# A two-layer decoder on one core: the index scores of all DSA blocks ahead, the three selections behind the rest of the first stage

## The chip, the core and the metric

The kernel runs on one core of one Trainium2 chip. The metric is the device time of one execution in microseconds (us). The engines are named as in the profile: PE is TensorE (PEld its weight loads), DVE is VectorE, ACT is ScalarE, POOL is GpSimd, and SP is SyncE, which here only issues DMAs. Each engine works through its own queue in order; semaphores make one engine wait for another.

## The reference, cut to what matters

The reference is a decoder of two layers over 512 positions of width 1024. Each layer projects its input with one wide matrix and gives the columns to four mixers (`hgrn2`, `dsa`, `nsa`, `mlstm`); their outputs are joined and projected back, and cross-attention and a gated feed-forward follow. The change touches the `dsa` mixer only. For each block of 128 queries that mixer scores all keys with a small index network, keeps the 128 best keys of each query, and attends over those alone:

```python
topk = min(DSA_TOPK_MAX, l_ // 4)          # 128
def block(bi):
    rel = jax.nn.relu(jnp.einsum('bthd,bsd->bhts', iqb, ik))     # 8 index heads of 32
    score = jnp.einsum('bhts,bth->bts', rel, iwb).astype(F32)
    score = jnp.where(causal[None], score, -jnp.inf)
    _, idx = lax.top_k(score, topk)
    ...
```

A query of block 0 has at most 128 causal keys, so block 0 needs no selection. Blocks 1, 2 and 3 have 256, 384 and 512 causal keys to choose from.

## The kernel before, in words

The matrices are multiplied in split form: an operand is a pair of tiles, a rounded part and the rest (`xh` and `xl`, `wh` and `wl`), and a product is three matmuls. Weights come by DMA (`raw_tile`, L277), ACT makes the rounded part (L292) and POOL the rest (L293). In the second layer the first stage's weights come already split (L303).

`run` takes each layer through stages. The first stage holds, side by side, `dsa` (index scores and selections), `nsa_in` and `nsa`, `ml_in` and `ml`, and the projections `ml_in2`, `dsa_in2` and `hg_in`. The second stage holds `dsa_attn`, `hg` and the output projections; it reads the selections' masks, and its pools `hg`, `dat` and `xT` take the place of the first stage's pools `ml` and `nsa`.

Two things set the order of the work. First, the work is written as generators that are woven by `mix`: each part has a total, each `yield` names a cost, and the part whose spent share of its total is smallest goes on. `dsa` followed by `hg_space` is one part with a total of 74; everything else of the first stage is the other, with a total of 225. Second, Tile's planner lays out the queues (`schedule_with_timeline_sim=True`): what was emitted earlier has priority, and an engine that is free in its plan takes the best instruction that is ready then. `first()` moves weight loads, splits and some evictions far ahead. The queues that result are fixed in the program; on the chip an instruction that isn't ready holds up all behind it on its engine.

Inside `dsa`, for each block in turn, `index(tb)` makes the split query tile `iqs` (two ACT copies, one POOL subtract, L668 to L670), transposes it on PE into PSUM `dt` and copies it out as `iqT` (L497), then for each of 8 heads does one matmul (L679), one ACT relu into `rel` (L681) and one DVE pass that adds the weighted head into the score tile `iacc` (L684, L685, L688). `select(tb)` then runs 16 rounds on that tile: `max` finds the 8 largest of a row (L696) and `match_replace` overwrites them (L697); one more instruction makes the mask `dmask` (L700). There is one `iacc` tile (bufs=1), one `iqs` and one `iqT`, so a block's scores can only be added up once the selection before is done. The matmuls of `index` and its transposes share one PSUM bank, `dt`, through an alias.

After the selections `hg_space` closes the pool `dsa` and opens `hgin`. Only then may `hg_in` write its last two projections, `hgi` and `hgg`, into `h_v` and `h_g` (L485); it loops in `while self.hin is None` until then.

The last piece of the first stage is the last head of `ml`: four products into the single PSUM bank `mb` (L1048), each read by a DVE pass into `m_p` (L1056), then 20 matmuls (L1065), a chain of small DVE instructions on `m_den` (L1069 to L1079) and the output `mo`.

Of the kernel before, what the change touches and what calls it, by code (L numbers as in the profile page):

```python
# [7 lines left out]
FT = mybir.dt.float32  # L8
FR = mybir.dt.float32r
BF = mybir.dt.bfloat16  # L10
U8 = mybir.dt.uint8
AF = mybir.ActivationFunctionType
OP = mybir.AluOpType
# [193 lines left out]
class Kernel:  # L207
# [434 lines left out]
    def dsa(self, pool, keep):  # L642
        nc = self.nc
        idx = self.d_idx
        st = self.t(pool, "d_st", [128, 64], bufs=1)

        ik = idx[:, :, 256:288]
        self.sumsq(st[:, 4:8], ik, pool)
        self.rsqrt(pool, st[:, 8:12], st[:, 4:8], 1.0 / 32, EPS)
        self.tt(ik, ik, st[:, 8:12, None].to_broadcast([128, TB, 32]), OP.mult)  # L650
        self.tt(ik, ik, self.row("idxk_gain")[:, None, :].to_broadcast([128, TB, 32]), OP.mult)
        self.rope(idx[:, :, 256:288].rearrange("p t (h d) -> p t h d", h=1), self.ic, self.isn, 4, pool)
        iq = idx[:, :, 0:256].rearrange("p t (h d) -> p t h d", h=8)
        self.rope(iq, self.ic, self.isn, 4, pool)
        iks = self.t2(pool, "iks", [128, TB, 96], FR)
        nc.vector.tensor_copy(iks[:, :, 0:32], ik)
        nc.vector.tensor_copy(iks[:, :, 32:64], ik)
        self.tt(iks[:, :, 64:96], ik, iks[:, :, 0:32].bitcast(FT), OP.subtract)
        ikT = self.t(pool, "ikT", [128, S], FR, bufs=1)
        self.transpose_blocks(ikT[0:96], lambda j: iks[:, j, :].bitcast(FT), TB, nc.vector.tensor_copy, rows=96,  # L660
                              pool=pool)

        yield 4.0

        def index(tb):
            n = (tb + 1) * 128
            iqs = self.t(pool, "iqs", [128, 8, 96], FR, bufs=1)
            nc.scalar.activation(iqs[:, :, 0:32], iq[:, tb], AF.Copy)  # L668
            nc.scalar.activation(iqs[:, :, 64:96], iq[:, tb], AF.Copy)
            self.tt(iqs[:, :, 32:64], iq[:, tb], iqs[:, :, 0:32].bitcast(FT), OP.subtract, nc.gpsimd)  # L670
            iqT = self.t(pool, "iqT", [128, 8, 128], FR, bufs=1)
            for g in range(2):
                self.transpose_blocks(iqT[0:96, 4 * g:4 * g + 4].rearrange("p a b -> p (a b)"),
                                      lambda j: iqs[:, 4 * g + j, :].bitcast(FT), 4, self.act_copy, rows=96,
                                      pool=pool)
            acc = self.t(pool, "iacc", [128, S], bufs=1)[:, :n]
            for h in range(8):
                sc = self.psum("sc", pool=pool)
                nc.tensor.matmul(sc[:, :n], iqT[0:96, h], ikT[0:96, :n], start=True, stop=True)  # L679
                rel = self.t2(pool, "rel", [128, S])  # L680
                nc.scalar.activation(rel[:, :n], sc[:, :n], AF.Relu, scale=1.0 / 16)  # L681
                w = idx[:, tb, 288 + h:289 + h]
                if h == 0:
                    nc.vector.tensor_scalar(acc[:, :n - 128], rel[:, :n - 128], w, None, op0=OP.mult)  # L684
                    nc.vector.scalar_tensor_tensor(acc[:, n - 128:n], rel[:, n - 128:n], w, self.k("neg"),  # L685
                                                   op0=OP.mult, op1=OP.add)
                else:
                    nc.vector.scalar_tensor_tensor(acc, rel[:, :n], w, acc, op0=OP.mult, op1=OP.add)  # L688
                yield 0.7
            return acc  # L690

        def select(tb, acc, masks):
            n = (tb + 1) * 128
            m8 = self.t(pool, "m8", [128, 8])
            for r in range(16):
                nc.vector.max(m8, acc)  # L696
                nc.vector.match_replace(acc, m8, acc, -3e38)  # L697
                yield 0.4 + 0.25 * tb
            masks[tb] = self.t(keep, f"dmask{tb}", [128, n], BF, bufs=1)
            nc.vector.tensor_scalar(masks[tb], acc, -2e38, NEG, op0=OP.is_gt, op1=OP.mult)  # L700

        masks = self.d_masks = {0: None}
        for tb in range(1, TB):
            acc = yield from index(tb)
            yield from select(tb, acc, masks)

    def dsa_attn(self, pool):
        nc, l = self.nc, self.l
# [828 lines left out]
    def run(self):  # L1537
        nc = self.nc
        late = ExitStack()
        for l in range(DEPTH):  # L1540
            self.l = l
            banks = ExitStack()
            self.banks(banks, "ba", tp=1, sc=2, o=1, dt=1, mb=1)
            if l == 0:
                self.load_x(self.i["xT"])
            self.layer_consts()
            if l == 0:
                self.open_sq()
            right, index = ExitStack(), ExitStack()
            self.hqf = self.pool(right, "hgqf", side="right")  # L1550
            self.mo = {2: self.t(self.mp, "mo2", [128, 2, S], bufs=1), 3: self.t(self.mp, "mo3", [128, TB, 256], bufs=1)}
            pd = self.pool(index, "dsa", n2=4, n4=0, side="right")
            self.alias[id(pd)] = {"tp": "dt", "sc": "dt"}
            acc = self.dsa_in(pd)
            if l == 0:
                self.setup()
            self.rstd(row=True)
            if l == 0:
                xd = self.i["xT"]
            else:  # L1560
                xd = self.tc.dram_tile([D, S], FT, name=f"xd{l}")
                for c in range(KC):
                    nc.sync.dma_start(xd[c * 128:c * 128 + 128, :], self.xT[c])
            self.xpool.close()
            late.close()
            late, left = ExitStack(), ExitStack()
            pk = self.pool(late, "keep")
            pm = self.pool(left, "ml", n2=3)
            pn = self.pool(left, "nsa", n2=3, n4=1)
            self.alias[id(pn)] = {}  # L1570
            self.hin = None
            for tb in range(TB):
                with self.first():
                    nc.scalar.activation(self.d_idx[:, tb], acc[tb], AF.Copy, scale=self.rcol[:, tb:tb + 1])
            self.weave((self.chain(self.dsa(pd, pk), self.hg_space(index, right)), COST["dsa"]),
                       (self.chain(self.nsa_in(pn),
                                   self.mix((self.nsa(pn), COST["nsa"]),
                                            (self.chain(self.ml_in(pm),
                                                        self.mix((self.ml(pm), COST["ml"]),
                                                                 (self.chain(self.ml_in2(pm), self.dsa_in2(pk), self.hg_in()), COST["in"]))),  # L1580
                                             COST["mlin"]))),
                        COST["two"]))
            left.close()
            banks.close()
            banks = ExitStack()
            self.banks(banks, "bb", tp=1, sc=1, o=1, dt=1, hb=2)
            self.load_x(xd)
            ph = self.pool(left, "hg", n2=2, n4=0)
            pa = self.pool(left, "dat", n2=3, n4=0)
            px = self.pool(right, "xk", n2=2, n4=1, side="right")  # L1590
            self.alias[id(pa)] = {"tp": "dt"}
            self.attn_done = False
            self.weave((self.dsa_attn(pa), COST["attn"]), (self.hg(ph), COST["hg"]),
                       (self.chain(self.out_stage(0), self.xa_kv(px), self.out_stage(1)), COST["out"]))
            left.close()
            banks.close()
            banks = ExitStack()
            self.banks(banks, "bc", tp=2, sc=2, o=2)
            self.open_sq()
            with ExitStack() as e:  # L1600
                p = self.pool(e, "xa")
                rest = self.xa_in(p)
                right.close()
                self.raws = (self.pool(right, "raw", side="right"), RAWS)
                self.all(self.xa(p, self.pool(e, "xo", side="right"), rest))
            with ExitStack() as e:
                self.ffn(self.pool(e, "ffn"))
            self.raws = (self.wp, 3)
            right.close()
            banks.close()  # L1610
        self.xpool.close()
        late.close()
# [18 lines left out]
```

## Time and profile before

| what | value |
|---|---|
| time, median of 3 runs (lowest to highest) | 1689.66 us (1684.8 to 1689.67) |
| profiled execution: its time | 1688.9 us |
| profiled execution: its span | 1687.1 us |
| outside the span in that execution | 1.8 us |
| PE busy, share of the span | 1607.5 us (95%) |
| DVE busy | 924.0 us (55%) |
| ACT busy | 712.5 us (42%) |
| POOL busy | 799.1 us (47%) |
| mean granted TensorE clock | 0.972 |

The profile is one execution. Its page gives busy times, the span in 40 slices, and the groups of instructions; the trace behind it answers for any stretch, line or tile. A busy PE is not PE at its peak, since matmuls are pipelined and their ends are modelled. Idle time of an engine that isn't the bottleneck costs nothing. The granted clock is a share of full speed: 1.0 is 2.4 GHz, and half of that is the other level, 1.2 GHz; a mean between the two is a stretch that had both. In the trace the first stage of the first layer runs from about 25 to 277 us, that of the second layer from about 877 to 1115 us.

### The profile page before, as it was taken

How to read it: one execution, taken by the hardware profiler on the slowest of the kernel's cores; microseconds unless marked ns; L12 is line 12 of the kernel's file. 1: busy time of each engine (PE TensorE's matmuls, PEld its weight loads, DVE VectorE, ACT ScalarE, POOL GpSimd, SP SyncE). 2: the span in 40 equal slices, each digit the busy share in tenths (PEclk: the TensorE clock that was granted, in tenths of full speed). 3: DMA queues.
4: the chain of work that ended last, by engine and by line, in shares of the span. 5: the costliest groups of instructions: out<-in, count | busy, mean ns of one | idle time of the engine just before them, and what ended most of it. 6: DMA issues, size and time to landing. Idle time of an engine off the chain costs nothing.

```text
span 1687.1 us, 25484 instructions
## 1 busy us (share of the span) xinstructions
PE 1607.5 (95%) x9256; PEld 1333.1 (79%) x9262; DVE 924.0 (55%) x1760; ACT 712.5 (42%) x1525; POOL 799.1 (47%) x698
## 2 busy tenths in 40 slices
PE   7899998998899989999999999989998999999999
PEld 7778877777788868888898887677877888888887
DVE  5697688876755330344225884879786644123420
ACT  5555453454654443443324433423665433223321
POOL 5664333456448888874412010144672344444442
PEclk9999997999999999999999999979999999999999
DMA  5342212212338999953355734122131233333331
GB/s 160 89 119 76 70 34 84 57 38 85 112 121 286 305 316 319 333 192 93 105 156 178 262 107 132 58 95 57 45 119 38 66 97 90 92 100 94 94 103 66
DMA packets 114365, 212.72 MB, mean 126 GB/s; under 512 B 12984, under 2 KB 30136, under 8 KB 114240
## 3 DMA queue, kind: packets, MB, share of 16 engines
q1 hardware_dynamic: 111888, 206.11, 38.7%
q10 hardware_dynamic: 2032, 3.94, 0.7%
q8 instruction: 73, 1.20, 0.3%
q0 software_dynamic: 320, 1.05, 0.2%
q14 instruction: 52, 0.43, 0.1%
HBM read 170.69 MB, written 40.35 MB: 125 GB/s over the span
## 4 chain that ended last, share of the span: by engine, by line
PE 84%; DVE 8%; issue 3%; DMA 2%; POOL 2%; ACT 2%; SPq 0%; POOLq 0%; ACTq 0%; DVEq 0%
PE acc L329 14%; PE acc L331 14%; PE acc L330 14%; PE sc L330 5%; PE sc L331 5%; PE sc L329 5%; PE acc L339 3%; PE acc L340 3%; PE acc L341 3%; PE hb L856 3%; PE o L574 2%; PE sc L552 2%; PE tp L493 2%; PE mb L1048 1%; PE dt L493 1%
## 5 line engine op out<-in xcount | busy, mean ns | idle before, releaser
L293 POOL TENSOR_TENSOR wl<-wr,wh 128x512 fp32r<-128x512 f32 (+5 forms) x432 | 551.7, 1285 | 459.3 <-ACT wh L292 447.8
L292 ACT ACTIVATE wh<-wr 128x512 fp32r<-128x512 f32 (+5 forms) x432 | 252.1, 592 | 336.2 <-PE acc L330 149.2
L329 PE MATMUL acc<-xh,wh 128*128 128x512 f32 (+1 forms) x704 | 276.9, 395 | 0.8 <-ACT xh L1283 0.5
L330 PE MATMUL acc<-xl,wh 128*128 128x512 f32 (+1 forms) x704 | 274.6, 390 | 2.9 <-DVE xl L1277 2.9
L331 PE MATMUL acc<-xh,wl 128*128 128x512 f32 (+1 forms) x704 | 275.4, 392 | 0.4 <-POOL wl L293 0.4
L466 DVE TENSOR_TENSOR xT<-acc,xT 128x512 f32<-128x512 f32 (+1 forms) x112 | 68.1, 611 | 214.4 <-PE acc L331 213.6
L329 PEld LDWEIGHTS acc<-xh,wh 128*128 128x128 f32 x704 | 133.9, 191 | 32.1 <-issue 1.7
L330 PEld LDWEIGHTS acc<-xl,wh 128*128 128x128 f32 x704 | 134.3, 191 | 30.8 <-DVE xl L1277 4.0
L331 PEld LDWEIGHTS acc<-xh,wl 128*128 128x128 f32 x704 | 134.1, 190 | 28.7 <-POOL wl L293 1.1
L329 PE MATMUL acc<-f_gh,wh 128*128 128x512 f32 x352 | 139.1, 397 | 6.8 <-ACT f_gh L1491 6.8
L339 PE MATMUL acc<-wh,xh 128*128 128x256 f32 (+2 forms) x480 | 140.6, 296 | 4.9 <-DMA wh<-whl 3.8
L331 PE MATMUL acc<-f_gh,wl 128*128 128x512 f32 x352 | 139.7, 398 | 0.7 <-POOL wl L293 0.7
L330 PE MATMUL sc<-xl,wh 128*128 128x512 f32 x352 | 139.7, 397 | 0.0
L330 PE MATMUL acc<-f_gl,wh 128*128 128x512 f32 x352 | 139.5, 398 | 0.0
L340 PE MATMUL acc<-wl,xh 128*128 128x256 f32 (+2 forms) x480 | 139.0, 291 | 0.0
L331 PE MATMUL sc<-xh,wl 128*128 128x512 f32 x352 | 139.0, 395 | 0.0
L329 PE MATMUL sc<-xh,wh 128*128 128x512 f32 x352 | 138.0, 393 | 0.0
L341 PE MATMUL acc<-wh,xl 128*128 128x256 f32 (+2 forms) x480 | 137.4, 288 | 0.0
L318 POOL TENSOR_TENSOR phl<-pr,phl 128x512 fp32r<-128x512 f32 (+3 forms) x72 | 95.1, 1321 | 35.0 <-ACT phl L317 31.8
L317 ACT ACTIVATE phl<-pr 128x512 fp32r<-128x512 f32 (+3 forms) x72 | 44.2, 613 | 133.9 <-DMA pr<-in_wst 117.2
L339 PEld LDWEIGHTS acc<-wh,xh 128*128 128x128 f32 x480 | 92.9, 194 | 8.8 <-DMA wh<-whl 4.3
L340 PEld LDWEIGHTS acc<-wl,xh 128*128 128x128 f32 x480 | 93.3, 195 | 1.4 <-issue 0.8
(407 smaller groups left out, 3159.8 us busy)
## 6 DMA issues: line engine op xcount, KB each, us to landing
wr<-in_wst SPq DMA_DIRECT2D x332, 256.0 KB, 2.7
whl<-phl SPq DMA_DIRECT2D x52, 512.0 KB, 3.9
pr<-in_wst SPq DMA_DIRECT2D x52, 256.0 KB, 4.1
wh<-whl SPq DMA_DIRECT2D x52, 256.0 KB, 4.1
wl<-whl SPq DMA_DIRECT2D x52, 256.0 KB, 4.4
wr<-in_wst SPq DMA_DIRECT2D x48, 128.0 KB, 2.2
wr<-in_wst SPq DMA_DIRECT2D x32, 192.0 KB, 2.4
whl<-phl SPq DMA_DIRECT2D x8, 524.0 KB, 3.7
```

Of the source, the lines that this page charges most:

```text
L292: nc.scalar.activation(hi, raw, AF.Copy)
L293: nc.gpsimd.tensor_tensor(lo, raw, hi.bitcast(FT), op=OP.subtract)
L318: nc.gpsimd.tensor_tensor(both[:, 1], raw, both[:, 0].bitcast(FT), op=OP.subtract)
L329: self.nc.tensor.matmul(acc, wh, xh, start=(j == 0), stop=False)
L330: self.nc.tensor.matmul(acc, wh, xl, start=False, stop=False)
L331: self.nc.tensor.matmul(acc, wl, xh, start=False, stop=(j == n - 1))
L339: self.nc.tensor.matmul(acc, xh[:, s], wh, start=(first and j == 0), stop=False)
L340: self.nc.tensor.matmul(acc, xh[:, s], wl, start=False, stop=False)
L341: self.nc.tensor.matmul(acc, xl[:, s], wh, start=False, stop=(last and j == n - 1))
L466: self.nc.vector.tensor_add(self.xT[c][:, cols], acc, self.xT[c][:, cols])
L493: self.nc.tensor.transpose(p[:rows, j * 128:j * 128 + 128], src(j), self.ident)
L856: nc.tensor.matmul(sc[s0:s1, b + t0:b + t1], kk[po:po + 64, b + s0:b + s1], qq[po:po + 64, b + t0:b + t1], start=True, stop=True)
```

## The change: what it does

- `index` is called for blocks 1, 2 and 3 before any selection. Each block has a score tile of its own (`iacc1` to `iacc3`).
- `index` works in two halves of four heads: `iqs` and `iqT` are half as large, and `iqT` has two buffers. A head's `yield` is 0.5 in place of 0.7.
- After the last index head there is a `yield 60.0`. At that point `dsa` has spent 4 + 24 x 0.5 + 60 = 76 of its total of 74, so `mix` goes on with the other part until that has spent 76/74 of 225, which is 231.
- The 16 rounds follow, in each round blocks 1, 2 and 3 one after the other, each with its own `m8` tile; then the three masks.
- `hg_space`, and with it `hgi` and `hgg`, still comes behind the selections.
- The pool `dsa` has three buffers of the tag `t2` (`rel` and others) in place of four.

```diff
+        accs = {tb: self.t(pool, f"iacc{tb}", [128, (tb + 1) * 128], bufs=1) for tb in range(1, TB)}
+
         def index(tb):
             n = (tb + 1) * 128
-            iqs = self.t(pool, "iqs", [128, 8, 96], FR, bufs=1)
-            nc.scalar.activation(iqs[:, :, 0:32], iq[:, tb], AF.Copy)
-            nc.scalar.activation(iqs[:, :, 64:96], iq[:, tb], AF.Copy)
-            self.tt(iqs[:, :, 32:64], iq[:, tb], iqs[:, :, 0:32].bitcast(FT), OP.subtract, nc.gpsimd)
-            iqT = self.t(pool, "iqT", [128, 8, 128], FR, bufs=1)
+            acc = accs[tb]
             for g in range(2):
-                self.transpose_blocks(iqT[0:96, 4 * g:4 * g + 4].rearrange("p a b -> p (a b)"),
-                                      lambda j: iqs[:, 4 * g + j, :].bitcast(FT), 4, self.act_copy, rows=96,
-                                      pool=pool)
-            acc = self.t(pool, "iacc", [128, S], bufs=1)[:, :n]
-            for h in range(8):
...
-                yield 0.7
-            return acc
-
-        def select(tb, acc, masks):
-            n = (tb + 1) * 128
-            m8 = self.t(pool, "m8", [128, 8])
-            for r in range(16):
-                nc.vector.max(m8, acc)
-                nc.vector.match_replace(acc, m8, acc, -3e38)
-                yield 0.4 + 0.25 * tb
-            masks[tb] = self.t(keep, f"dmask{tb}", [128, n], BF, bufs=1)
-            nc.vector.tensor_scalar(masks[tb], acc, -2e38, NEG, op0=OP.is_gt, op1=OP.mult)
-
+
+                four = iq[:, tb, 4 * g:4 * g + 4]
+                iqs = self.t(pool, "iqs", [128, 4, 96], FR, bufs=1)
+                nc.scalar.activation(iqs[:, :, 0:32], four, AF.Copy)
+                nc.scalar.activation(iqs[:, :, 64:96], four, AF.Copy)
+                self.tt(iqs[:, :, 32:64], four, iqs[:, :, 0:32].bitcast(FT), OP.subtract, nc.gpsimd)
+                iqT = self.t(pool, "iqT", [128, 4, 128], FR, bufs=2)
+                self.transpose_blocks(iqT[0:96].rearrange("p a b -> p (a b)"), lambda j: iqs[:, j, :].bitcast(FT), 4,
+                                      self.act_copy, rows=96, pool=pool)
+                for h in range(4 * g, 4 * g + 4):
+                    sc = self.psum("sc", pool=pool)
+                    nc.tensor.matmul(sc[:, :n], iqT[0:96, h % 4], ikT[0:96, :n], start=True, stop=True)
...
+                    yield 0.5
+
+        for tb in range(1, TB):
+            yield from index(tb)
+
+        yield 60.0
+        for r in range(16):
+            for tb in range(1, TB):
+                m8 = self.t(pool, f"m8{tb}", [128, 8])
+                nc.vector.max(m8, accs[tb])
+                nc.vector.match_replace(accs[tb], m8, accs[tb], -3e38)
+                yield 0.05
         masks = self.d_masks = {0: None}
         for tb in range(1, TB):
-            acc = yield from index(tb)
-            yield from select(tb, acc, masks)
+            masks[tb] = self.t(keep, f"dmask{tb}", [128, (tb + 1) * 128], BF, bufs=1)
+            nc.vector.tensor_scalar(masks[tb], accs[tb], -2e38, NEG, op0=OP.is_gt, op1=OP.mult)
...
-            pd = self.pool(index, "dsa", n2=4, n4=0, side="right")
+            pd = self.pool(index, "dsa", n2=3, n4=0, side="right")
```

## Rows read from the trace of the kernel before

**Rows 1.** Windows: stretch, length, busy of each engine (instructions), clock, DMA share.
```profile
42.00:126.00 84.00, 72.87 (x512) 64.31 (x511) 65.39 (x143) 47.60 (x113) 52.05 (x39) 0.95 0.36 102
126.00:252.00 126.00, 124.93 (x825) 100.41 (x824) 93.06 (x193) 65.93 (x149) 47.44 (x38) 0.99 0.21 61
252.00:277.00 25.00, 17.88 (x85) 13.87 (x84) 22.80 (x60) 5.84 (x15) 3.81 (x5) 0.60 0.00 1
...
984.00:1092.00 108.00, 106.99 (x706) 85.17 (x706) 71.32 (x174) 40.83 (x95) 9.75 (x8) 1.00 0.29 96
1092.00:1115.00 23.00, 16.63 (x86) 14.47 (x87) 20.96 (x53) 6.49 (x16) 3.88 (x9) 0.70 0.01 1
```

**Rows 2.** Timeline of DVE: start, length; the last mask of each layer.
```profile
274.08 0.43 DVE L700 TENSOR_SCALAR dmask<-iacc 128x512 bf16<-128x512 f32 x1
...
1109.92 0.43 DVE L700 TENSOR_SCALAR dmask<-iacc 128x512 bf16<-128x512 f32 x1
```

**Rows 3.** Waits of PE from 252 to 277 us: total us, times, longest.
```profile
PE tp L1281 <- DVE mo L351: 2.5, 1, 2.5
PE mb L1048 <- DVE m_p L1056: 2.1, 2, 1.3
PE dt L723 <- DVE rs_ms L347: 1.0, 1, 1.0
```

**Rows 4.** Waits of PE from 1092 to 1115 us, the second layer's end.
```profile
PE mb L1048 <- DVE m_p L1056: 3.4, 2, 2.7
PE dt L1161 <- DVE mo L351: 1.9, 1, 1.9
PE mb L1048 <- DVE mo L351: 1.0, 1, 1.0
```

**Rows 5.** Timeline of PE: one head's 20 matmuls of L1065, at three places.
```profile
263.90 4.53 PE L1065 MATMUL mb<-m_v,m_p 128*128 128x65 f32 x20 [0.38 <-DVE m_p L1056]
...
1086.32 2.34 PE L1065 MATMUL mb<-m_v,m_p 128*128 128x65 f32 x20
...
1103.20 4.53 PE L1065 MATMUL mb<-m_v,m_p 128*128 128x65 f32 x20 [0.68 <-DVE m_p L1056]
```

**Rows 6.** Windows of line L696 alone (max): DVE busy (instructions), clock; the sum.
```profile
126.00:252.00 126.00, 12.42 (x22) 0.99 0.21 61
252.00:277.00 25.00, 7.59 (x11) 0.60 0.00 1
...
984.00:1092.00 108.00, 12.65 (x21) 1.00 0.29 96
...
sum 450.00, DVE 53.52; mean DVE 8.92
```

**Rows 7.** The same windows of line L697 alone (match_replace).
```profile
126.00:252.00 126.00, 13.58 (x42) 0.99 0.21 61
252.00:277.00 25.00, 8.23 (x22) 0.60 0.00 1
...
984.00:1092.00 108.00, 13.95 (x43) 1.00 0.29 96
...
sum 450.00, DVE 59.11; mean DVE 9.85
```

**Rows 8.** Timeline of POOL near the start: an instruction emitted late that runs early.
```profile
3.63 0.17 POOL L1222 MEMSET n_kbd<- 128x64 f32 x1
```

**Rows 9.** Waits of PE over the whole span, those on the index chain.
```profile
PE dt L679 <- ACT iqT L497: 3.2, 2, 2.6
PE dt L493 <- ACT rel L681: 3.1, 1, 3.1
...
PE dt L493 <- ACT iqT L497: 2.5, 2, 1.8
```

**Rows 10.** Two lines of DVE, whole span: count, shortest, median, longest ns.
```profile
L696 DVE MAX8 m<-iacc x96: 397/561/696, 79.5 to 1108.4; 128x8 f32<-128x256 f32 x32, 128x8 f32<-128x384 f32 x32, 128x8 f32<-128x512 f32 x32
...
L1008 DVE SCALAR_TENSOR_TENSOR m_y<-m_x,cols,m_y x24: 731/752/1872, 122.2 to 1065.9; 128x512 f32<-128x512 f32 x24
```

More of the change, by code (lines that the diff above doesn't have):

```diff
@@ L672, in index @@
-            for g in range(2):
-                self.transpose_blocks(iqT[0:96, 4 * g:4 * g + 4].rearrange("p a b -> p (a b)"),
-                                      lambda j: iqs[:, 4 * g + j, :].bitcast(FT), 4, self.act_copy, rows=96,
-                                      pool=pool)
-            acc = self.t(pool, "iacc", [128, S], bufs=1)[:, :n]
-            for h in range(8):
[L678 to L688, printed above, removed]
-                yield 0.7
@@ new lines, in index @@
+            for g in range(2):
+                four = iq[:, tb, 4 * g:4 * g + 4]
[9 more added lines that the diff above has]
+                    nc.tensor.matmul(sc[:, :n], iqT[0:96, h % 4], ikT[0:96, :n], start=True, stop=True)
+                    rel = self.t2(pool, "rel", [128, S])
+                    nc.scalar.activation(rel[:, :n], sc[:, :n], AF.Relu, scale=1.0 / 16)
+                    w = idx[:, tb, 288 + h:289 + h]
+                    if h == 0:
+                        nc.vector.tensor_scalar(acc[:, :n - 128], rel[:, :n - 128], w, None, op0=OP.mult)
+                        nc.vector.scalar_tensor_tensor(acc[:, n - 128:n], rel[:, n - 128:n], w, self.k("neg"),
+                                                       op0=OP.mult, op1=OP.add)
+                    else:
+                        nc.vector.scalar_tensor_tensor(acc, rel[:, :n], w, acc, op0=OP.mult, op1=OP.add)
+                    yield 0.5
```

## The prediction, made before the changed kernel was run

> **What bounds the kernel now.** I read the page first: PE is busy for 95% of the span and DVE for 55%. On average the kernel is bound by PE, and an edit to DVE's work is worth nothing unless some stage differs from the average. So I asked for windows. In the middle of the first stage PE is busy all the time and DVE has room: from 126 to 252 us PE works 124.93 of 126 us and DVE 93.06, and in the second layer, from 984 to 1092, PE 106.99 of 108 and DVE 71.32 [rows 1]. At the end of the stage the two change places: from 252 to 277 us DVE works 22.80 of 25 us and PE 17.88, from 1092 to 1115 DVE 20.96 of 23 and PE 16.63, and there alone the granted clock falls, to means of 0.60 and 0.70, between its two levels of 2.4 and 1.2 GHz [rows 1]. PE had waited in those stretches before it fell.
>
> What fills DVE there is the third selection: the last masks are made at 274.08 and 1109.92 us, 2.5 and 4.7 us before the stretches end [rows 2]. In the first layer 7.59 us of `max` and 8.23 us of `match_replace` lie in the 25 us of the tail, together 15.8 us [rows 6, 7]. They sit in DVE's queue between the last head's instructions. So PE waits for `m_p`, for `mo` and for a small `rs_ms`, 5.6 us in the largest three [rows 3], and in the second layer 6.3 us for `m_p` and `mo` [rows 4]. After the waits it runs at the lower clock: the 20 matmuls of L1065 take 4.53 us at either end and 2.34 us for the head before [rows 5].
>
> Why is the third selection so late? Block 3 can't add up its scores before block 2's selection has freed the one score tile, and its index work was emitted behind that selection.
>
> **The change part by part.**
>
> *Rounds out of the tail.* Nothing of the rounds is removed: 53.52 us of `max` and 59.11 us of `match_replace` in the two layers, so 56.3 us in each [rows 6, 7]. They are emitted last, so in the planner's list they are the filling for whatever DVE leaves free. That the planner does fill with work emitted far behind is seen at 3.63 us, where POOL clears a tile of `nsa_cmp` that is used much later [rows 8]. What room is there? In the middle of the first layer DVE's work other than rounds is 93.06 - 12.42 - 13.58 = 67.1 us, which leaves 126 - 67.1 = 58.9 us; in the second layer 71.32 - 12.65 - 13.95 = 44.7 us and 63.3 us [rows 1, 6, 7]. Both are above the 56.3 us wanted, and both are low counts: the score passes of blocks 2 and 3, which leave these stretches, are still in them, and from 42 to 126 us DVE has another 84 - 65.39 = 18.6 us idle [rows 1], open to the first blocks' rounds. Rounds beside a busy PE cost it nothing so far: 22 `max` and their partners lie in a stretch in which PE idles for 1.1 of 126 us [rows 1, 6]. So I take the rounds to be done before 252 and 1092 us, and their price in the middle as nothing. If the cover fails, each of the 96 wide instructions of a layer can push back what is queued behind it on DVE (the `stat` reduction that the attention's exponentials wait for, `m_p`, the evictions of `proj_T`) by up to its length; that is the second rival.
>
> The gain: the waits, 5.6 + 6.3 = 11.9 us [rows 3, 4], and the slowed L1065, 2 x (4.53 - 2.34) = 4.4 us [rows 5], together 16.3 us. The least is 0, if the bare chain of products and `m_p` makes PE wait as long and the clock falls all the same; the most is all of PE's idle time in the two stretches, (25 - 17.88) + (23 - 16.63) = 13.5 us, and the clock's share of its busy time, 0.40 x 17.88 + 0.30 x 16.63 = 12.1 us, together 25.6 us [rows 1]. I take 16.3, the sum of waits with a name.
>
> What is late next? The last head's own chain, and with it the second stage, whose pools wait for the first stage's. `hgi` and `hgg`, eight projections, stay behind `hg_space`; once the rounds are planned early, that pool opens early and they become filling for PE's holes in the tail. That is the way to the upper end.
>
> *Index work ahead.* Sixteen heads and 16 transposes of a layer move from the middle, where PE has no idle time, towards the front, where it idles for 84 - 72.87 = 11.1 us [rows 1]. PE's sum is the same. Part of that idle time is the index chain itself: at the passage from one block to the next PE waits 3.2, 3.1 and 2.5 us for `iqT` and `rel`, 8.8 us in the two layers [rows 9]. Now a second such passage, from block 2 to block 3, comes into the front, where there is less other work; against it, the halves are shorter and `iqT` has two buffers, so the next transposes need not wait for the last head. Bounds: the 8.8 us go, or they come twice. I take 0, and keep +/-8.8.
>
> *Smaller instructions.* 24 ACT copies of half the size and 12 POOL subtracts in place of 12 and 6 in the two layers: no row prices the halves, so at the most they cost what 12 and 6 more would; ACT has 84 - 47.60 = 36.4 us idle in the front and POOL 32.0 [rows 1]. Nothing. The `rel` pool of three buffers lets ACT run three heads ahead of DVE in place of four; the front's DVE time covers it. The change adds no DMA. SP's queue keeps its order; the loads of the second stage, gated by the first stage's last tiles, start earlier by what the tail loses.
>
> *POOL beside DVE.* A selection that moves from the tail, where POOL works 3.81 of 25 us, to the middle, where it works 47.44 of 126 [rows 1], could be slowed by it. The rows say no for the rounds: `max` ran 96 times between 397 and 696 ns at three widths, while the two-tile pass of L1008 has a median of 752 ns and a longest of 1872 [rows 10]. The Trainium skill (SBUF — State Buffer, section "Who interferes with whom") states the same split: a DVE instruction with two SBUF inputs can be shut out for the whole of a GpSimd instruction that reads SBUF, one with a single input can't. By that rule the score passes, which read two tiles, are the ones to fear: 14 of them come into the first layer's front, where POOL works 52.05 of 84 us, and at L1008's worst surcharge of 1.1 us each that is 15.7 us of DVE. DVE's idle 18.6 us there takes it up, so the sum stays; all of it on PE's path would end at 1672.6 + 15.7 = 1688.3 us.
>
> **The sum.** Profiled execution 1688.9 us (span 1687.1 and 1.8 around it; the median of the runs is 0.8 above): 1688.9 - 16.3 = 1672.6 us.
>
> **The rivals.**
>
> 1. *PE fills the tail.* `hgi` and `hgg` run in the holes and the clock stays up: the gain is 25.6 us, 1663.3. For it: they are PE work without a DVE input. Against it: the last head's chain of DVE and PE steps has its own length and the second stage waits for its end.
>
> 2. *The rounds don't find their room* (slower). The planner lays the queues by its own durations; where it sees DVE busier than it is, rounds pile up at the stage's end, and there `hg_space`, `hgi`, `hgg` and the masks wait behind them. The point from which it decides: the tail holds 15.8 us of rounds now, so it gets worse when more than that is left of 56.3, and more than the 2.2 us that DVE idles there take up [rows 1]: when fewer than 56.3 - 18.0 = 38.3 of the 58.9 us are used, 65%. At 45% (26.5 us used) 29.8 us are left, 14.0 more than now, in two layers 28.0 us; DVE's idle 2.2 and 2.0 us in the tails [rows 1] take up 4.2: 1688.9 + 23.8 = 1713. At 60% 21.0 us are left and it is 1688.9 + 2 x (21.0 - 15.8) - 4.2 = 1695. For it: all rounds are now last in rank, where only the third selection was late before. Against it: DVE's room was used densely before, and rounds can start at the front.
>
> 3. *The front takes it back.* The passages stall PE twice as long, 8.8 us, and pull the clock down after: 1672.6 + 8.8 = 1681.4, and with half of the tail's gain 1689.5, no change.
>
> **How the numbers follow.** A measurement of this kernel can tell about 0.3% from no change, 5 us. Chances: the forecast 0.50 (1672.6), rival 1 0.14 (1663), rival 3 0.18 (1681 to 1690, half of it within 0.3% of before), rival 2 0.18 (1695 to 1713). Faster: 0.50 + 0.14 + 0.09 = 0.73, less 0.03 for a forecast whose front loses its whole bound and more; same 0.12; slower 0.18. The range: from 1688.9 - 25.6 - 8.8 = 1654.5 at the low end to 1694 at the high end, which leaves out most of rival 2 and the best of both fronts together.
>
> **What would show it.** In the changed kernel the last `dmask` should lie well before the tail; the window of the tail should show DVE half idle and the clock near 1.0; the waits for `m_p` and `mo` should be under 1 us each, and L1065's last head near 2.3 us. PE's waits for `iqT` and `rel` tell of the front, and 126 to 252 us should still show PE without idle time. I am wrong if rounds stand next to each other after the last head, if DVE is the releaser of PE's waits in the middle, or if the front's window shows PE below 72 of 84 us.

## The result, and the profile after

The changed kernel takes 1705.6 us (median of four runs; 1687.2 for the kernel before, beside it on the same chip). The ratio is 1.0134, with a 95% interval of 1.0091 to 1.0177: slower by 1.3%, where I had forecast 1672.6. One of the four runs took 1727.0 us and pulls the ratio up; the medians lie 18.3 us apart, 1.1%. A run in the chip's slower state is left out of the ratios of this document, but not out of the medians. The profiled execution took 1705.3 us with a span of 1703.5.

In the changed kernel most line numbers are 2 to 7 higher: the heads' product is L682, the relu L684, the score pass L691, `max` L701, `match_replace` L702, the mask L707, `m_p` L1058, the 20 matmuls L1067.

First the stretches of [rows 1] and the fronts. The changed kernel's first stage ends later, so its real tail and the 42 us from its last `mo` pass on come behind them, each with a stretch of its own. Columns: stretch, length, busy time of PE, PEld, DVE, ACT and POOL (instructions), granted clock, DMA share, GB/s. The changed kernel:

```profile
42.00:126.00 84.00, 69.69 (x464) 59.77 (x463) 64.94 (x152) 48.47 (x118) 42.06 (x34) 0.90 0.30 88
126.00:252.00 126.00, 117.56 (x748) 93.76 (x748) 86.42 (x199) 58.38 (x131) 49.40 (x39) 0.92 0.24 65
252.00:277.00 25.00, 25.00 (x195) 21.74 (x194) 9.07 (x17) 14.21 (x31) 12.31 (x9) 1.00 0.22 58
...
1092.00:1115.00 23.00, 23.00 (x178) 19.46 (x177) 7.63 (x12) 9.88 (x23) 3.88 (x4) 1.00 0.24 81
...
84.00:168.00 84.00, 68.09 (x434) 54.05 (x435) 78.65 (x207) 50.32 (x125) 35.58 (x30) 0.81 0.26 73
924.00:1008.00 84.00, 69.35 (x437) 53.54 (x436) 78.06 (x203) 42.81 (x113) 9.01 (x12) 0.82 0.47 158
277.00:302.50 25.50, 23.96 (x163) 20.91 (x162) 10.63 (x29) 9.33 (x21) 8.59 (x8) 0.95 0.19 51
302.50:344.50 42.00, 36.66 (x191) 28.73 (x190) 36.19 (x74) 13.29 (x32) 21.88 (x27) 0.91 0.33 105
1115.00:1143.50 28.50, 27.34 (x205) 23.87 (x204) 11.62 (x29) 11.67 (x26) 11.70 (x10) 1.00 0.21 66
1143.50:1185.50 42.00, 37.29 (x198) 29.37 (x198) 39.09 (x79) 11.47 (x26) 22.86 (x31) 0.88 0.28 88
```

The kernel before, in the fronts and in the 42 us from its last `mo` pass on:

```profile
84.00:168.00 84.00, 80.19 (x546) 67.41 (x547) 71.28 (x161) 48.69 (x124) 45.19 (x36) 0.94 0.34 98
924.00:1008.00 84.00, 81.36 (x562) 67.97 (x563) 68.88 (x185) 36.06 (x102) 5.69 (x8) 0.96 0.56 193
275.90:317.90 42.00, 38.22 (x260) 33.67 (x260) 34.99 (x70) 17.09 (x40) 23.07 (x29) 0.90 0.35 109
1113.60:1155.60 42.00, 38.21 (x256) 33.98 (x256) 34.19 (x61) 12.62 (x25) 23.26 (x28) 0.92 0.41 126
```

The tail did what I forecast, but not at the old times. From 252 to 277 and from 1092 to 1115 us PE now works all of 25 and 23 us at full clock, where it had 17.88 and 16.63, and DVE is more than half idle. The last masks lie far ahead of the places in [rows 2]. These two stretches, though, are no longer the tail: the last head's last `mo` pass comes 26.6 and 29.9 us later than before. In the real tail, from 277 to 302.5 and from 1115 to 1143.5 us, PE idles 1.5 and 1.2 us, and the clock is at 0.95 and 1.00. Timeline of DVE, the last masks and the last `mo` pass of each layer, in the changed kernel:

```profile
185.03 0.43 DVE L707 TENSOR_SCALAR dmask<-iacc 128x512 bf16<-128x512 f32 x1
302.45 0.42 DVE L351 TENSOR_TENSOR mo<-mo,m_tok 128x256 f32<-128x256 f32 x1
1030.28 0.43 DVE L707 TENSOR_SCALAR dmask<-iacc 128x512 bf16<-128x512 f32 x1
...
1143.50 0.42 DVE L351 TENSOR_TENSOR mo<-mo,m_tok 128x256 f32<-128x256 f32 x1
```

The last `mo` pass of each layer in the kernel before:

```profile
275.87 0.42 DVE L351 TENSOR_TENSOR mo<-mo,m_tok 128x256 f32<-128x256 f32 x1
...
1113.64 0.42 DVE L351 TENSOR_TENSOR mo<-mo,m_tok 128x256 f32<-128x256 f32 x1
```

The last head's matmuls take 2.45 and 2.34 us where [rows 5] has 4.53. Timeline of PE, the last head of each layer in the changed kernel:

```profile
295.51 2.45 PE L1067 MATMUL mb<-m_v,m_p 128*128 128x65 f32 x20 [0.45 <-DVE m_p L1058]
...
1137.15 2.34 PE L1067 MATMUL mb<-m_v,m_p 128*128 128x65 f32 x20
```

The loss is at the front. Between 84 and 168 us PE works 68.09 us where it had worked 80.19, between 924 and 1008 us 69.35 in place of 81.36: 12 us less in each layer, and the clock falls to 0.81 and 0.82. From the last `mo` pass on, the second stage begins hardly worse than before: PE works 1.6 and 0.9 us less of 42. `hgi` and `hgg` are now done ahead of that pass and no longer lie beside that start.

A sum over each layer, from the first stage's first evictions to the cross-attention's first product, needs no stretches that match. The kernel before (28.4 to 445.4 and 877.7 to 1295.8 us), then the changed one (27.5 to 450.6 and 882.5 to 1312.1):

```profile
sum 835.10, PE 782.09 PEld 657.39 DVE 616.24 ACT 399.11 POOL 341.12; mean PE 391.05 PEld 328.69 DVE 308.12 ACT 199.55 POOL 170.56
sum 852.70, PE 787.48 PEld 655.36 DVE 599.82 ACT 402.61 POOL 340.66; mean PE 393.74 PEld 327.68 DVE 299.91 ACT 201.30 POOL 170.33
```

PE's idle time rises from 53.0 to 65.2 us, by 12.2. The two fronts alone lose 24.1, so elsewhere PE idles 11.9 us less than before. The other 5.4 us are longer busy time: the mean clock of the two layers falls from 0.95 and 0.96 to 0.94.

What PE waits for at the front (total us, times, longest), from 84 to 168 us and then from 924 to 1008:

```profile
PE dt L682 <- ACT rel L684: 5.0, 5, 1.6
PE tp L521 <- DVE n_hs L351: 4.7, 1, 4.7
...
PE dt L682 <- ACT rel L684: 4.5, 6, 1.4
PE tp L521 <- DVE n_hs L351: 3.9, 1, 3.9
```

And the place itself, in the timeline of PE:

```profile
127.13 0.80 PE L682 MATMUL dt<-ikT,iqT 96*128 96x512 f32 x1 [0.69 <-ACT rel L684]
129.18 0.80 PE L682 MATMUL dt<-ikT,iqT 96*128 96x512 f32 x1 [1.26 <-ACT rel L684]
130.73 0.79 PE L682 MATMUL dt<-ikT,iqT 96*128 96x512 f32 x1 [0.75 <-ACT rel L684]
132.21 0.47 PE L1202 MATMUL dt<-kc,n_hid 64*128 64x64 f32 x2 [0.69 <-ACT rel L684]
137.37 1.09 PE L521 MATMUL tp<-kc,qd 128*128 128x128 f32 x4 [4.68 <-DVE n_hs L351]
```

Two things are to be seen. The heads of block 3 stand alone: one matmul, then PE waits until ACT has read the bank. And right behind the last head comes L1202, a transpose of `n_hid`, the compression of `nsa`, which works in the same bank `dt`; in the kernel before that transpose ran at 104.3 us, here at 132.2. Behind it PE stands for 4.68 us at L521. That line reads the query tile `qd` and nothing of `n_hs`. The profile puts the wait down to `n_hs` since that ended last, but what PE needs is the copy of `qd` right ahead of it on DVE. (In the kernel with block 2 alone ahead, below, the profile itself names `qd` for a wait of 3.9 us at L521.) What DVE did in those 4.68 us:

```profile
132.44 0.72 DVE L691 SCALAR_TENSOR_TENSOR iacc<-rel,d_idx,iacc 128x512 f32<-128x512 f32 x1
...
133.83 0.53 DVE L702 MATCH_REPLACE8 iacc<-m,iacc 128x384 f32<-128x384 f32 x1
134.39 2.58 DVE L1182 COPY n_blk<-n_kv 64x496 f32<-64x496 f32 x2
137.00 0.23 DVE L1129 COPY qd<-n_qr 128x128 f32<-128x128 f32 x1
137.14 0.22 DVE L351 TENSOR_TENSOR n_hs<-dt,n_hs 128x64 f32<-128x64 f32 x1
```

It worked without a pause on a round, a score pass and other parts' tiles; the short copy of `qd` was queued behind them. Below, "the wait at L521" is this one.

### The profile page after: what moved, and what is told of

The parts are those of the page before. It is cut to its first block, busy times and chain, and to the rows that moved or that the text cites. A ratio compares the mean times of both kernels' runs of the same rounds, so it can differ in the third digit from the quotient of the medians.

```text
span 1703.5 us, 25535 instructions
## 1 busy us (share of the span) xinstructions
PE 1612.1 (95%) x9262; PEld 1331.3 (78%) x9262; DVE 905.1 (53%) x1760; ACT 715.6 (42%) x1537; POOL 799.1 (47%) x704
## 4 chain that ended last, share of the span: by engine, by line
PE 67%; DVE 7%; POOL 3%; DMA 2%; issue 2%; ACT 2%; SPq 0%; POOLq 0%; ACTq 0%; DVEq 0%
PE acc L329 12%; PE acc L330 12%; PE acc L331 12%; PE sc L330 5%; PE sc L331 5%; PE sc L329 4%; PE acc L339 2%; PE acc L340 2%; PE acc L341 2%; PE hb L858 2%; PE tp L493 1%; PE o L574 1%; POOL wl L293 1%; PE sc L552 1%; DMA pr<-in_wst 1%
## 5 line engine op out<-in xcount | busy, mean ns | idle before, releaser
L293 POOL TENSOR_TENSOR wl<-wr,wh 128x512 fp32r<-128x512 f32 (+5 forms) x432 | 544.9, 1270 | 493.1 <-ACT wh L292 462.1
```

The source lines that it names most:

```text
L293: nc.gpsimd.tensor_tensor(lo, raw, hi.bitcast(FT), op=OP.subtract)
```

## The experiments

**Rounds left out, in either order.** Does the front lose because of the rounds (theory 1) or of the index work (theory 2)?

```diff
-                nc.vector.max(m8, accs[tb])
-                nc.vector.match_replace(accs[tb], m8, accs[tb], -3e38)
```

> The changed kernel with its 96 max and match_replace of a layer left out (the masks are made from the bare scores, so the result is not the reference's); every yield stays. In the changed kernel PE idles 15.9 us between 84 and 168 us (before: 3.8) and about 14.6 between 924 and 1008. Theory 1, the rounds: bunched in the middle they keep DVE at 41.5 of 42 us there and hold up what PE waits for. Then that idle time falls to about 4 us in each layer and the time to about 1705.6 - 2 x 12 = 1682 or below. Theory 2, the index work: three blocks' heads run one behind the other on the one bank dt, and PE waits for relu after relu whatever DVE does. Then PE's idle time there stays above 12 us and the time above 1698.

> The kernel before with the rounds left out in the same way (masks from the bare scores, not the reference's result). It prices the rounds in the old order. If the tail's waits were all they cost, as my sum had it, it gives 1687.2 - 16.3 = 1671, between 1662 and 1680. If the price in the old order was larger (they also hold something in the middle), it falls below 1662. By theory 1 the changed kernel without rounds comes within 5 us of this one; by theory 2 it stays about 17 above it.

Measured: 1692.2 us for the changed order (ratio to the kernel before 1.0012, 0.9991 to 1.0032) and 1667.9 for the old one (0.9852, 0.9779 to 0.9926). The 1692 lies between the two expectations. The fronts of that kernel, without a round in the program:

```profile
84.00:168.00 84.00, 72.20 (x431) 57.12 (x430) 46.79 (x100) 50.66 (x127) 34.01 (x30) 0.77 0.27 79
924.00:1008.00 84.00, 71.11 (x468) 56.36 (x466) 49.29 (x107) 42.64 (x112) 10.00 (x12) 0.86 0.48 163
```

DVE now has 37 and 35 us to spare there, and PE still idles 11.8 and 12.9 us, where theory 1 wanted about 4 and theory 2 over 12. PE's waits from 42 to 200 us, rounds left out:

```profile
PE dt L682 <- ACT rel L684: 7.0, 7, 1.7
...
PE tp L521 <- DVE n_hs L351: 0.9, 1, 0.9
```

The long wait at L521 was the rounds' and is gone. The waits for `rel` have nothing to do with them.

By the medians the rounds cost 1688.4 - 1667.9 = 20.4 us in the old order and 1705.6 - 1692.2 = 13.4 in the new one, and the index work ahead costs 1692.2 - 1667.9 = 24.2 us with no round in the program. The four runs of the second kernel are 1656.0, 1657.4, 1678.5 and 1684.6 us, so these figures are rough. By the ratios the index work ahead costs 1.6%, 27 us, and an estimate from the two intervals puts it between 14 and 40. That it costs time without any rounds is clear of the noise. That the change saves 7.0 us of the rounds' cost, the difference of 20.4 and 13.4, is not.

**One half of the change at a time.** The index ahead, with the selections one block at a time right behind it; then the rounds last, with the index where it was (a head's `yield` at 0.7 again). Both diffs are against the changed kernel:

```diff
-        yield 60.0
-        for r in range(16):
-            for tb in range(1, TB):
...
+        masks = self.d_masks = {0: None}
+        for tb in range(1, TB):
+            m8 = self.t(pool, f"m8{tb}", [128, 8])
+            for r in range(16):
...
+                yield 0.4 + 0.25 * tb
```

> Half of the change: index of all blocks ahead into own tiles, in halves, but the selections follow at once and block by block with the old yields of 0.4 + 0.25 x block, not behind all else. Theory 1 (rounds emitted last are bunched in the middle): much of the loss goes, 1690 or below. Theory 2 (index of three blocks at the front): the loss stays, 1698 or more, with PE waiting for rel and iqT between 84 and 168 us.

```diff
         for tb in range(1, TB):
             yield from index(tb)
+            yield {1: 10.4, 2: 14.4, 3: 30.4}[tb]
-        yield 60.0
```

> The other half: the rounds last as in the change, but the index work of blocks 2 and 3 emitted where it stood before (heads at 0.7, and yields of 10.4 and 14.4 between the blocks in the place of the selections' costs). Theory 1: the rounds are still bunched, 1698 or more, DVE above 40 of 42 us in one stretch of the middle. Theory 2: the front is as before and the tail is clear, so the forecast's gain comes out, 1671 to 1681.

Measured: 1707.9 us (1.0122, 1.0084 to 1.0161) and 1688.1 us (1.0004, 0.9985 to 1.0023). All of the loss is with the index ahead. The second kernel was a miss for both theories: theory 2 had expected 1671 to 1681 from a tail that is clear. Where the rounds are emitted makes no difference in either: with the selections at once the last masks are made at 188.47 and 1029.31 us, as in the changed kernel, and with the rounds last they stay in the tail. In the second kernel the last mask of the first layer is made at 275.05 us. Its heads of blocks 2 and 3 in that layer (instructions; shortest, median and longest ns; first and last start):

```profile
L682 PE MATMUL dt<-ikT,iqT x16: 336/412/687, 84.2 to 242.5; 96*128 96x384 f32 x8, 96*128 96x512 f32 x8
```

Its tail, as a window:

```profile
252.00:277.00 25.00, 15.88 (x80) 12.96 (x77) 23.85 (x63) 5.10 (x14) 5.50 (x12) 0.64 0.09 28
```

Block 3 has a score tile of its own there, and its last head still runs at 242.5 us (before: 240.0). The kernel before with the rounds left out says the same: nothing of block 2's selection can hold up block 3 there, and its last head still runs at 236.8 us. The planner starts rounds when there are scores. The second kernel also has the halves of `iqs` and `iqT` and the three buffers of `t2`, so all of these together with the rounds last are priced: nothing.

**What in the index work costs: the bank.** Theory A: `dt` is one buffer, handed out in the order of emission, so heads that are emitted ahead lock the compression of `nsa` out. Theory B: it is PE's standing between the heads. Theory C: the bank doesn't matter. Against the changed kernel, first the scores go to the two `sc` banks; then, with the index work untouched, the two products of the compression go to `tp`:

```diff
-            self.alias[id(pd)] = {"tp": "dt", "sc": "dt"}
+            self.alias[id(pd)] = {"tp": "dt"}
```

> The changed kernel, with the index scores in the two sc banks that nsa's attention uses, not in the one bank dt (the transposes stay in dt). Index ahead without its rounds cost 24 us (1692.2 against 1667.9), with rounds 18. Theory A: the single bank is handed out in the order of emission, and the heads, now emitted ahead, keep nsa's compression out of dt until the last head (first n_hid transpose at 132.2 us, before 104.3). Theory B: PE stands between the heads, since each waits for the relu of the one before on the one bank (rel 6.4 us). Theory C: neither; index work at the front pushes everything else back whatever the bank. A and B both say that the loss shrinks, to 1697 or below, and that the 4.7 us for n_hs and the waits for rel go. C says 1702 or more.

```diff
-            p = self.psum("dt", (128, 2, 64))
+            p = self.psum("tp", (128, 2, 64))
...
-            p = self.psum("dt", (128, 64))
+            p = self.psum("tp", (128, 64))
```

> The changed kernel, with the two products of nsa's compression (n_hid transposes, n_cmp) moved from the bank dt to tp; the index work is not touched. Theory A (the heads keep the compression out of dt): the first n_hid transpose goes back from 132 to about 105 us, the wait for n_hs goes, and at least half of the loss, to 1697 or below. Theory B (PE stands between heads): the waits for rel stay at 4 to 7 us in each layer and the time at 1702 or more. Theory C: 1702 or more with neither wait explaining it.

Measured: 1695.1 us (1.0029, 1.0000 to 1.0059) and 1690.7 us (1.0010, 0.9980 to 1.0039). With the scores on `sc` the wait at L521 is gone, `n_hid` starts at 113.7 us, and the waits for `rel` fall from 6.4 and 4.5 to 3.6 and 3.2 us in the two layers, as A and B both said. In the second kernel two lines that touch nothing of the index work take back 14.9 us of the 18.3, and PE works 76.02 and 78.18 us of the two fronts, where the changed kernel has 68.09 and 69.35. The wait at L521 is gone there too. The first layer's heads and `n_hid` transposes in the second kernel, then in the changed one:

```profile
L682 PE MATMUL dt<-ikT,iqT x16: 338/478/796, 83.7 to 143.5; 96*128 96x384 f32 x8, 96*128 96x512 f32 x8
L1202 PE MATMUL tp<-kc,n_hid x4: 223/247/271, 113.1 to 151.7; 64*128 64x64 f32 x4
```

```profile
L682 PE MATMUL dt<-ikT,iqT x15: 338/502/796, 85.5 to 130.7; 96*128 96x512 f32 x8, 96*128 96x384 f32 x7
L1202 PE MATMUL dt<-kc,n_hid x4: 214/269/366, 132.2 to 154.6; 64*128 64x64 f32 x4
```

On `tp` the compression starts at 113.1 us, amid the heads, which now end later, at 143.5. It didn't get back to 105: `tp` has other users. The waits for `rel` between 42 and 200 us fell as well, from 6.4 to 3.7 us, since PE has other work between the heads. So B is for a good part a result of A. What the two lines do to the kernel before, alone, wasn't run; with block 3 spread (below) they cost time, so the 14.9 us are what the bank gives here and no price for the bank in general. The Trainium skill (PSUM — Partial Sum Buffer, section "PSUM bank collisions raise a hardware error") says that two engines can't use one PSUM bank within the same partition at the same time, and that semaphores have to guard a bank. The trace agrees: the last heads in `dt` wait 0.69 to 1.26 us each for the relu that reads the bank. The order in which the bank's users follow each other is not from there but from the program: in the changed kernel no transpose of `n_hid` lies between two heads of blocks 2 and 3.

**Only block 2 ahead, without and with the other bank.** The diff is against the kernel with the rounds last alone; the second run has the two lines for `tp` as well.

```diff
-            yield {1: 10.4, 2: 14.4, 3: 30.4}[tb]
+            yield {1: 0.0, 2: 24.8, 3: 30.4}[tb]
```

> Rounds last; only block 2's index work is put ahead, right behind block 1's, block 3's stays where it stood before (emitted behind nsa's compressed branch). Theory A: the compression waits for 16 heads in place of 8, its first transpose lies near 115 us, and part of the loss comes without any of the tail's gain: 1692 to 1700. Theory B the same for 8 heads of the waits for rel. If it stays within 3 us of the kernel before, block 2 is not the cause and all of the loss is block 3's.

> Block 2 ahead (1702.4), with the compression on tp. In the fully changed kernel this took back 15 of the 18 us. Theory A: the same here, 1686 to 1693. Theory C (index work at the front itself, whatever the bank): 1698 or more, and the 15 us that tp gave in the full change came from block 3's heads alone.

Measured: 1702.4 us (1.0087, 1.0062 to 1.0113) and, with the compression on `tp`, 1688.3 us (1.0011, 0.9991 to 1.0031). Block 2 alone, ahead, loses 16 us, more than I had expected for a transpose that comes at 115.3 us; its third masks still come at 267.96 and 1110.23 us, and PE works 19.07 and 17.64 us of the tails of [rows 1], hardly more than before. The other bank returns 14 of the 16. The two pairs agree on the bank's share.

**Block 3 between the steps of `nsa`.** If only the order in `dt` is to blame, block 3's heads can come earlier as long as they let `nsa` have turns. Again against the kernel with the rounds last alone; the runs that follow put 1.2 and 2.6 in the place of 1.9, and the last has the two lines for `tp`:

```diff
-            yield {1: 10.4, 2: 14.4, 3: 30.4}[tb]
+            yield {1: 10.4, 2: 0.0, 3: 30.4}[tb]
...
-                    yield 0.7
+                    yield 0.7 if tb < 3 else 1.9
```

> Rounds last; blocks 1 and 2 indexed where they stood before, block 3 begun right behind block 2 but its heads 1.9 apart, so that they are emitted between the steps of nsa's compressed branch and take turns with them on dt. Theory A: the scores of block 3 are done some 40 us sooner (before: heads at 208 to 240 us), nsa's chain is hardly held up, the third selection leaves the tail and the gain that I forecast comes out: 1671 to 1683. Theory C: what the tail gives is taken back before it, 1686 or more.

> Block 3's heads 1.2 apart in place of 1.9. Scores done earlier, rounds further from the tail, but more heads ahead of nsa's second compression on dt. Theory A: between the spread kernel and the changed one, 1672 to 1685. If it is below 1670, the tail still held what counts at 1.9.

> Block 3's heads 2.6 apart. Scores done later, more of the third selection back in the tail, less in nsa's way: 1672 to 1685 by theory A, towards the kernel before. Below 1670: dt in the middle still cost something at 1.9.

> The kernel with block 3 spread (1671.7), with nsa's compression on tp as well. Theory A: with the heads spread, the compression hardly waits for dt any more (first n_hid transpose at 102.8 us), so the other bank brings little: 1666 to 1674. If it brings another 10 us, dt was still the limit in the spread kernel; if it costs, tp is worse shared than dt.

Measured: 1671.7 us at 1.9 (0.9897, 0.9832 to 0.9963), 1672.3 at 1.2 (0.9923, 0.9898 to 0.9947), 1677.9 at 2.6 (0.9950, 0.9930 to 0.9969). These beat both kernels, by about 1% and 2% in the first two. At 1.9, the heads of blocks 2 and 3 and `n_hid` in the first layer:

```profile
L682 PE MATMUL dt<-ikT,iqT x16: 338/394/483, 85.0 to 224.3; 96*128 96x384 f32 x8, 96*128 96x512 f32 x8
L1202 PE MATMUL dt<-kc,n_hid x4: 222/247/275, 102.8 to 166.7; 64*128 64x64 f32 x4
```

The last `mo` pass of each layer in the same kernel, timeline of DVE:

```profile
271.88 0.42 DVE L351 TENSOR_TENSOR mo<-mo,m_tok 128x256 f32<-128x256 f32 x1
...
1099.35 0.42 DVE L351 TENSOR_TENSOR mo<-mo,m_tok 128x256 f32<-128x256 f32 x1
```

The heads end 16 us sooner than before, the first `n_hid` starts no later (the last one does, at 166.7 us for 149.4), no head's matmul is stretched to 0.80 us, and the first stage's last `mo` pass comes 4.0 and 14.3 us sooner than before. The expectation of 40 us sooner was wrong; the third selection still reaches the tail (its masks are made at 267.77 and 1095.45 us), and the time came out as expected all the same. The other two spacings lie in the range that theory A gave them.

What the spread alone is worth isn't shown. These kernels also leave block 2 where it stood, and block 2 put ahead costs 16 us by itself. Block 3 in one piece with block 2 in its old place wasn't run, and 1.2 did as well as 1.9.

The compression on `tp` in this kernel was a miss: 1695.2 us (1.0019, 0.9980 to 1.0057), where theory A said 1666 to 1674. Its `n_hid` transposes start at 111.7 us, 9 later than on `dt`: here `tp`, with its own users, is the later bank. That fits the sign, but doesn't explain the size: three of its ten times lie from 1676.6 to 1678.3 us and seven from 1694.9 to 1702.1, the profile is of the shortest, and what the long ones lost isn't known.

## Why the prediction was wrong

*The tail* was right by each sign that I had named, once it is looked for where it now lies: the masks, DVE's idle half, the clock, the waits for `m_p` and `mo` (the longest 0.5 and 0.6 us after), the 20 matmuls. The gain was real, too: outside the two fronts PE idles 11.9 us less than before, and I had summed 11.9 us of waits. That the two agree to a tenth is chance, since the 11.9 us measured hold also what other stretches gained and lost. The slower clock that I wanted back in the tail was lost in the front. My reading that the clock falls in the tails alone was wrong as well: the front had 0.95 [rows 1], and from 84 to 168 us it was at 0.94.

*Why the third selection was late* was half wrong. I put it down to the single score tile and to the emission. The score tile doesn't matter: with a tile for each block and the index where it stood, block 3's last head runs at 242.5 us. Emission of the index decides, since it sets block 3's turn in `dt`.

*Rounds in the middle at a price of nothing*: they did find the room early, done at 185 and 1030 us, but not free. They cost 13.4 us in the new order by the medians, among it most of the waits of 4.7 and 3.9 us at L521, which are 0.9 and 0.6 us without rounds. My cover was PE's work, and that ran out: the rows on which I rested, 22 `max` beside a PE that idles 1.1 of 126 us [rows 1, 6], had PE fed, and in the changed kernel it idles 8.4 us of that stretch.

*Index work ahead at 0 +/- 8.8 us* is the step that failed: some 24 us without any rounds, 14 to 40 with the noise. I priced it by PE's waits for the index chain [rows 9], so by what the index work itself waits for, and didn't ask who waits for it. Those waits did stay in my bounds: 8.8 us before, 14.3 after, over the whole span. The loss lies with the others. I had written that the matmuls share the bank `dt`, but looked at that bank from the index's side alone. The trace of before showed the others in it: `n_hid` from 104.3 us on, among block 2's heads, and the rest of the compressed branch up to 192 us, ahead of block 3's heads at 208 to 240. A move of 16 heads to the front is a move past all of them, and giving two products of that branch another bank returned 14.9 of the 18.3 us.

*The rivals.* The third, that the front takes it back, had the place and the fall of the clock right, and a third of the size; it looked for the waits at the passages between blocks, and they lie between the heads of a block and at L521. The second named a loss of about the right size with a mechanism that didn't come: no rounds piled up at the end of the stage. My own alarms, DVE as a releaser of PE and the front below 72 of 84 us, are both seen above (4.7 us at L521; 69.69).

*What stays open.* Were `dt` all of it, the changed kernel with the compression on `tp` would lie below the kernel before by what the tail gives; at 1690.7 us it doesn't. Its fronts still have 4.2 and 3.2 us less of PE's work than before. That is left of the index work ahead, or is what `tp` costs in place of `dt`; the waits for `rel` that are left (3.7 us and 1.7 us in the two layers) are a part of it, the rest has no name. Whether `hgi` and `hgg`, held back, would help the second stage's start wasn't tried.

## What to carry to other kernels

A buffer that has one copy is a queue: list all who use it, in the order in which they use it, before moving one of them, and price the move by who then waits, not by what the moved work waits for. Work put ahead to free a late stage can be spread between the steps of the chain that owns the bank; here sixteen heads ahead in one piece gave a loss of 1.3%, and eight of them a few steps apart, with the others left in place, a gain of 1%. When a change moves the end of a stage, look for that stage by its last instruction and not by the old times. Where a planner fills holes by itself, emitting work last doesn't make it late: it starts as soon as its inputs exist, so move the inputs.

## What the runs showed of the hardware

How long the clock stays low after a wait differs widely, and in one trace 30 us of busy PE didn't end it. In the changed kernel PE waits 2.84 us for `xT` near 322 us, and the clock is at 0.50 for one stretch of 5 us:

```profile
320.00:325.00 5.00, 2.16 (x10) 1.49 (x9) 5.00 (x7) 1.05 (x2) 3.42 (x3) 0.90 0.28 90
325.00:330.00 5.00, 5.00 (x13) 3.83 (x14) 3.36 (x8) 0.06 (x1) 3.39 (x4) 0.50 0.12 19
330.00:335.00 5.00, 5.00 (x29) 3.96 (x28) 4.19 (x10) 1.17 (x2) 1.55 (x2) 0.92 0.10 37
```

With the compression on `tp`, a wait of 3.09 us for `h_aT` in the same part of the program is followed by more than 30 us at the lower level, with PE busy in all of it:

```profile
330.00:335.00 5.00, 2.24 (x9) 2.02 (x10) 4.74 (x14) 1.81 (x9) 0.61 (x1) 0.60 0.10 28
335.00:340.00 5.00, 5.00 (x20) 4.03 (x21) 2.68 (x5) 0.45 (x1) 1.62 (x2) 0.50 0.00 0
...
365.00:370.00 5.00, 5.00 (x25) 4.41 (x26) 1.72 (x4) 2.49 (x6) 1.62 (x2) 0.64 0.04 8
```

At half the clock 30 us of matmuls are 15 us lost, an estimate that takes PE for the limit in all of it; that is nearly the whole question of this study, from one wait of about the same size. That run was the longest of its ten (1697.6 us, median 1690.7), so the stretch need not be in the others. PE's work isn't the same in the two either: projections behind the first gap, mostly products of `hg` and of the attention behind the second. What decides between the two wasn't found out.

The heads of block 3 in the changed kernel are another case: the granted clock is at 0.50 in each stretch of 5 us from 120 to 145 us, with matmuls of 0.80 us and waits of 0.7 to 1.3 us between them. The first and the last of those stretches:

```profile
120.00:125.00 5.00, 2.82 (x10) 1.43 (x9) 5.00 (x12) 1.89 (x3) 0.00 (x0) 0.50 0.33 106
...
140.00:145.00 5.00, 4.63 (x21) 3.09 (x23) 5.00 (x14) 3.32 (x11) 1.13 (x2) 0.50 0.01 3
```

The Trainium skill (TensorE: Matmul & The Clock Gate, section "A second HAM failure mode: psum-queue depth-cycling") tells of another kernel, in bf16, where short idle gaps of PE between groups of matmuls that go through the PSUM banks in turn made the clock go back and forth. The trace here has the gaps, but one bank and no back and forth: the clock stays at the lower level through those 25 us. The means of 0.81 and 0.82 of the two fronts come from such stretches.
